# A hybrid decoder layer in f32: q as a ninth Strassen group, k and v with tokens on partitions

## The chip, the core and the metric

The kernel is one program on one core of one Trainium2 chip. A core has a matrix engine (PE, with PEld for its weight loads), a vector engine (DVE), a scalar engine (ACT), a general engine (POOL, which also issues DMAs in its own instruction stream) and a sync engine (SP, which only issues DMAs). The engines run their own instruction lists in order and wait for each other through semaphores. The metric is the device time of one execution in microseconds; lower is better.

## What is computed

The reference, cut to what matters (512 tokens, model width 2048, 16 query heads and 4 key heads of width 64, window 128):

```python
h = rms_norm(x, norm_gain)
z = h @ w_in                                   # columns: q k v g_attn c_b c_c c_h g_conv
q, k, v, g_attn, c_b, c_c, c_h, g_conv = jnp.split(z, SPLITS, axis=-1)
q = partial_rope(rms_norm(q, q_norm_gain), pos)     # per head; first 16 of 64 entries turn
k = partial_rope(rms_norm(k, k_norm_gain), pos)
y_attn = sliding_window_attention(q, k, v, sinks) * silu(g_attn)
y_conv = c_b * short_conv(c_c * c_h, conv_w) * silu(g_conv)
x = x + concatenate([y_attn, y_conv]) @ w_out
gate = sigmoid(rms_norm(x, ple_gate_norm_gain) @ w_ple_gate + b_ple_gate)
e = rms_norm(p @ w_ple_proj, ple_norm_gain)         # p: 512 x 256
out = x + gate * e
```

## The kernel before

**Three products for one.** Each f32 factor is split in a high part (a cast to fp32r on ACT) and a low part (the difference, on DVE). A product is three matmuls, high by high, high by low and low by high, 512 columns wide each. `wh` and `wl` are the parts of the weights, `hsh` and `hsl` those of h.

**Order.** Only PE's list is written out by hand throughout. In the first half of the program the other engines' lists are set by a scheduler (except for the first chunks); from the Strassen groups on all five lists stand in the order in which the code is written.

**First half.** (1) k and v: for each of 16 row blocks of x the block is scaled and split, and four tiles of k and v get three matmuls each, channels on partitions. (2) 16 tiles of 128 columns of w_in (`gemm_tile`, 48 matmuls each): eight of q, then eight of c_c and c_h. Between tiles lie, by a tick count (`at(when, fn)`, a tick is 6 matmuls), the attention of 16 pairs of key head and block, one `attention(j, n, when)` each, with `scores` at its tick, `turn` (transposes of the probabilities) 6 ticks later and `values` 9 ticks later. `q_tile` squares a tile of q, sums the squares per head by matmuls against `ind` (`half_sums`), turns them (`to_tokens`), and turns q by rope with four passes of DVE. (3) `e_block(n)`, the product of p and w_ple_proj, four times in the tiles of q. It needs the two tiles of p (`pt`), loaded through POOL's queue in `load_p` and split into `ptsh` and `ptsl`. (4) `h_forms` reads x again and makes, between the tiles, the sums of quarters of h that Strassen needs, and stores them in DRAM (`h_dram`).

**Second half.** Eight Strassen groups (`run_step`), 1024 columns of a product each: `g` 0 to 3 of w_in (the second halves of c_c and c_h; c_b and g_conv; g_attn), 4 and 5 of w_out, 6 and 7 of w_ple_gate. A group is 28 steps of 12 matmuls (7 products by 4 chunks) where the plain way takes 384. The weights of a step stand in the pools `wx`, `wy`, `ws`, are split two steps ahead (`prepare`), and their sums are made on DVE (`sums`) or by an accumulating DMA through POOL (`add_block`).

`rstd` makes 1 / sqrt on POOL, with an element-by-element power:

```python
nc.vector.tensor_scalar(ms, ms, 1.0 / n, EPS, op0=ALU.mult, op1=ALU.add)
nc.gpsimd.tensor_tensor(out, ms, e, op=ALU.pow)
```

Of the kernel before, what the change touches and what calls it, by code (L numbers as in the profile page):

```python
# [12 lines left out]
ALU = mybir.AluOpType  # L13

P = 128
# [12 lines left out]
NIN = 52  # L28
# [7 lines left out]
def hymba_layer(ctx: ExitStack, tc: tile.TileContext, io):  # L36
# [16 lines left out]
    ctx.enter_context(tc.manual_schedule(engines={mybir.EngineType.PE}))  # L53
# [5 lines left out]
    rowp = ctx.enter_context(tc.tile_pool(name="rowp", bufs=4, side="right", reuse_waits="tile"))  # L59
    ps_t = ctx.enter_context(tc.tile_pool(name="ps_t", bufs=2, space=PSUM))  # L60

    wide, early = ctx.enter_context(ExitStack()), ctx.enter_context(ExitStack())
    wsp = wide.enter_context(tc.tile_pool(name="wsp", bufs=4))
    wraw = wide.enter_context(tc.tile_pool(name="wraw", bufs=3))
    ps_g = wide.enter_context(tc.tile_pool(name="ps_g", bufs=2, space=PSUM, side="right"))
    big = early.enter_context(tc.tile_pool(name="big", bufs=31, side="right"))
    ps_s = early.enter_context(tc.tile_pool(name="ps_s", bufs=1, space=PSUM))
    ps_o = early.enter_context(tc.tile_pool(name="ps_o", bufs=1, space=PSUM))
    ps_m = early.enter_context(tc.tile_pool(name="ps_m", bufs=1, space=PSUM))
# [6 lines left out]

    E_AT = (2, 3, 4, 5)
    tiles = [TQ + i for i in range(8)]
    for i in range(4):
        tiles += [TCC + i, TCH + i]  # L80
    jobs = [io["w_kv"][i] for i in range(8)]
    for i, t in enumerate(tiles):
        jobs.append(io["w_in"][t, 0])
        if i in E_AT:
            jobs.append(io["w_ple_proj"][E_AT.index(i)])
        jobs.append(io["w_in"][t, 1])
    raws, splits = {}, {}
    RAW_AHEAD, SPLIT_AHEAD = 2, 3

    xt = []  # L90

    def load_x():
        xt.append(big.tile([P, T], F32, tag="big", name="x"))
        nc.sync.dma_start(xt[-1], io["x"][len(xt) - 1])

    def fetch(s):

        for j in range(min(s // 2 + RAW_AHEAD + 1, len(jobs))):
            if j not in raws:
                raws[j] = wraw.tile([P, 8, P], F32, name="raw")  # L100
                if j < 8:
                    for c in (slice(0, 4), slice(4, 8)):
                        nc.sync.dma_start(raws[j][:, c], jobs[j][:, c])
                        load_x()
                else:
                    nc.sync.dma_start(raws[j], jobs[j])

    def want(s, ahead):

        fetch(s)  # L110
        ahead = ahead if s > 5 else 0
        for j in range(min(s + ahead + 1, 2 * len(jobs))):
            if j not in splits:
                raw = raws[j // 2][:, (j % 2) * 4 : (j % 2) * 4 + 4]
                wh = wsp.tile([P, 4, P], F32R, name="wh")
                wl = wsp.tile([P, 4, P], F32R, name="wl")
                nc.scalar.copy(wh, raw)  # L117
                nc.vector.tensor_tensor(wl, raw, f32(wh), op=ALU.subtract)  # L118
                splits[j] = (wh, wl)
        return splits[s]  # L120

    tt, stt = nc.vector.tensor_tensor, nc.vector.scalar_tensor_tensor

    def split_tile(src, scale=None, name="s", pool=None):

        pool, tag = (big, "big") if pool is None else (pool, "h")
        h = pool.tile([P, T], F32R, tag=tag, name=name + "h")
        l = pool.tile([P, T], F32R, tag=tag, name=name + "l")
        if scale is None:
            nc.scalar.copy(h, src)  # L130
            nc.vector.tensor_tensor(l, src, f32(h), op=ALU.subtract)
        else:
            nc.scalar.activation(h, src, AF.Copy, scale=scale)
            nc.vector.scalar_tensor_tensor(l, src, scale, f32(h), op0=ALU.mult, op1=ALU.subtract)
        return h, l


    later = []
    clock = [0]

    def at(when, fn):
        later.append((when, len(later), fn))

    def tick():
        clock[0] += 1
        for item in sorted(x for x in later if x[0] <= clock[0]):
            later.remove(item)
            item[2]()

    def flush():  # L150
        while later:
            tick()

    def mm3(ps, wh, wl, ah, al, first, last):
        nc.tensor.matmul(ps, wh, ah, start=first, stop=False)  # L155
        nc.tensor.matmul(ps, wh, al, start=False, stop=False)  # L156
        nc.tensor.matmul(ps, wl, ah, start=False, stop=last)  # L157

    job = [0]

    def next_job(ahead=SPLIT_AHEAD):
        job[0] += 1
        return want(job[0] - 1, ahead)

    def gemm_tile(acts, mid=None):

        ps = ps_g.tile([P, T], F32, name="psg")
        for k in range(KT):
            if k == KT // 2 and mid:
                mid()  # L170
            if k % 4 == 0:
                wh, wl = next_job()
            ah, al = acts[k]
            mm3(ps, wh[:, k % 4, :], wl[:, k % 4, :], ah, al, k == 0, k == KT - 1)
            if k % 2:
                tick()
        return ps


    const.tile([P, 8], F32, name="pad")  # L180
    norm_g = const.tile([P, KT], F32, name="norm_gain")
    nc.scalar.dma_start(norm_g, io["norm_gain"])
    half_neg = const.tile([P, 32], F32, name="half_neg")
    nc.vector.memset(half_neg, -0.5)
    zeros = big.tile([P, P], F32, tag="big", name="zeros")
    nc.vector.memset(zeros, 0.0)
    nc.scalar.activation(half_neg[:, 31:], zeros[:, :1], AF.Copy, bias=-0.5)
    warm_ps = ps_o.tile([P, P], F32, name="pso")
    for _ in range(11):
        nc.tensor.matmul(warm_ps, zeros, zeros, start=True, stop=True)  # L190

    ind = const.tile([P, 2 * P], F32R, name="ind")
    for c in range(2):
        nc.vector.tensor_copy(ind[:, c * P : (c + 1) * P], zeros)
    ident = cload("ident", [P, P])
    gate_g = cload("ple_gate_norm_gain", [P, KT])
    qg, kg = cload("q_norm_gain", [P, 2]), cload("k_norm_gain", [P, 2])
    sink = cload("attn_sinks", [P, NH])
    convw = cload("conv_w", [P, 3, 8])
    nsink = const.tile([P, NH], F32, name="nsink")  # L200

    def half_sums(pm, hl, t, first, last):

        w = ind[:, P - 2 * t : 2 * P - 2 * t]
        nc.tensor.matmul(pm, w, hl[0], start=first, stop=False)
        nc.tensor.matmul(pm, w, hl[1], start=False, stop=last)

    def take_rows(pm, rows):
        sb = big.tile([rows, T], F32, tag="big", name="rowsum")
        nc.scalar.copy(sb, pm[:rows])  # L210
        return sb

    def to_tokens(sb):

        rows = sb.shape[0]
# [1201 lines left out]
```

## Time and profile before

| | |
|---|---|
| median of 3 runs | 937.83 us (936.92 to 941.45) |
| profiled execution | 936.5 us, its span 934.7 us |
| PE busy in the span | 922.9 us (99%) |
| DVE, ACT, POOL busy | 737.3, 533.5, 145.8 us |
| granted PE clock | 0.998 |
| moved by DMA | 188.22 MB |

The span runs from the first to the last instruction. "Busy" counts the time in which at least one instruction of an engine is under way, so that overlapping instructions count once. Matmuls overlap: one of 512 columns is under way for 390 ns, but the next starts long before it ends. A price per matmul is therefore read from the length of a run of them, not from the mean.

### The profile page before, as it was taken

The numbers are of one execution on the slowest core, as the hardware profiler recorded it, in microseconds if no ns is written. First come the engines' busy times: TensorE is split into PE (matmuls) and PEld (weight loads), VectorE is DVE, ScalarE is ACT, GpSimd is POOL, SyncE is SP. The second block draws the span as 40 slices with busy tenths as digits, with TensorE's granted clock in tenths as the row PEclk, the third lists the DMA queues.
The fourth block names the chain that finished last, engine by engine and source line by source line (L and its number), as shares of the span: only waits on it lengthen the run. The fifth ranks groups of instructions, "written<-read, shape, count | busy, mean of one in ns | idle before, by whom it ended". The sixth has DMA issues, their size and how long they took to land.

```text
span 934.7 us, 12298 instructions
## 1 busy us (share of the span) xinstructions
PE 922.9 (99%) x4264; PEld 765.9 (82%) x4264; DVE 737.3 (79%) x1115; ACT 533.5 (57%) x890; POOL 145.8 (16%) x190
## 2 busy tenths in 40 slices
PE   9999999999999899999999999999999999999997
PEld 8878888888888688888888888888888888888886
DVE  6776988888883877778667768989768696999778
ACT  7644856778883343445344446655657576565453
POOL 2002223154331000100100120011120112001100
PEclk9999999999999999999999999999999999999999
DMA  8524745556687677525924888795997996578747
GB/s 314 172 99 148 258 170 173 142 167 188 161 262 209 251 227 234 126 100 174 244 90 143 262 220 234 248 244 148 298 316 188 231 284 156 135 232 272 182 136 213
DMA packets 68590, 188.22 MB, mean 201 GB/s; under 512 B 8144, under 2 KB 14592, under 8 KB 68528
## 3 DMA queue, kind: packets, MB, share of 16 engines
q1 hardware_dynamic: 47312, 130.57, 40.6%
q0 software_dynamic: 21072, 56.86, 26.6%
q8 instruction: 33, 0.54, 0.2%
q14 instruction: 29, 0.24, 0.1%
q10 hardware_dynamic: 144, 0.01, 0.0%
HBM read 158.05 MB, written 29.36 MB: 200 GB/s over the span
## 4 chain that ended last, share of the span: by engine, by line
PE 96%; DVE 2%; issue 1%; ACT 0%; DVEq 0%
PE psp L853 60%; PE psg L155 6%; PE psg L156 6%; PE psg L157 6%; PE pst L853 3%; PE pss L276 2%; PE pst L276 2%; PE pst L919 2%; PE pst L484 1%; PE pss L564 1%; PE pst L564 1%; PE pss L451 1%; PE pss L452 1%; PE pso L499 1%; PE pso L498 1%
## 5 line engine op out<-in xcount | busy, mean ns | idle before, releaser
L853 PE MATMUL psp<-wh,form 128*128 128x512 f32 x1152 | 356.0, 390 | 0.0
L853 PEld LDWEIGHTS psp<-wh,form 128*128 128x128 f32 x1152 | 215.3, 188 | 44.1
L853 PE MATMUL psp<-wl,form 128*128 128x512 f32 x576 | 224.2, 389 | 0.0
L820 DVE TENSOR_TENSOR wl<-wy,wh 128x1024 fp32r<-128x1024 f32 x96 | 117.0, 1221 | 51.0 <-ACT wh L819 50.2
L819 ACT CAST wh<-wy 128x1024 fp32r<-128x1024 f32 x96 | 100.7, 1051 | 94.3 <-PE psp L853 69.3
L853 PEld LDWEIGHTS psp<-wl,form 128*128 128x128 f32 x576 | 108.1, 188 | 22.5
L820 DVE TENSOR_TENSOR wl<-wx,wh 128x1024 fp32r<-128x1024 f32 x64 | 78.1, 1222 | 40.8 <-ACT wh L819 40.6
L819 ACT CAST wh<-ws 128x1024 fp32r<-128x1024 f32 x64 | 67.5, 1054 | 71.6 <-PE psp L853 48.2
L819 ACT CAST wh<-wx 128x1024 fp32r<-128x1024 f32 x64 | 67.4, 1052 | 71.2 <-PE psp L853 58.5
L853 PE MATMUL psp<-wl,hsh 128*128 128x512 f32 x256 | 99.8, 390 | 3.4 <-DVE wl L820 3.4
L155 PE MATMUL psg<-hsh,wh 128*128 128x512 f32 x256 | 102.4, 400 | 0.0
L853 PE MATMUL psp<-wh,hsh 128*128 128x512 f32 x256 | 100.0, 391 | 0.0
L156 PE MATMUL psg<-hsl,wh 128*128 128x512 f32 x256 | 100.0, 391 | 0.0
L157 PE MATMUL psg<-hsh,wl 128*128 128x512 f32 x256 | 100.0, 390 | 0.0
L853 PE MATMUL psp<-wh,hsl 128*128 128x512 f32 x256 | 99.6, 389 | 0.0
L820 DVE TENSOR_TENSOR wl<-ws,wh 128x1024 fp32r<-128x1024 f32 x64 | 78.2, 1222 | 27.1 <-ACT wh L819 26.9
L805 DVE TENSOR_TENSOR wy<-wy,ws 128x1024 f32<-128x1024 f32 x64 | 77.9, 1218 | 0.0
L118 DVE TENSOR_TENSOR wl<-raw,wh 128x512 fp32r<-128x512 f32 x88 | 59.8, 685 | 17.7 <-PE pst L276 8.5
L117 ACT CAST wh<-raw 128x512 fp32r<-128x512 f32 x88 | 53.4, 614 | 30.2 <-PE psg L156 19.6
L853 PEld LDWEIGHTS psp<-wl,hsh 128*128 128x128 f32 x256 | 48.0, 188 | 13.8 <-DVE wl L820 3.8
L157 PEld LDWEIGHTS psg<-hsh,wl 128*128 128x128 f32 x256 | 48.1, 188 | 10.5
L853 PEld LDWEIGHTS psp<-wh,hsl 128*128 128x128 f32 x256 | 48.1, 188 | 9.9
(232 smaller groups left out, 1401.1 us busy)
## 6 DMA issues: line engine op xcount, KB each, us to landing
raw<-in_w_in SPq DMA_DIRECT2D x32, 512.0 KB, 3.7
ws<-in_w_mid SPq DMA_DIRECT2D x32, 512.0 KB, 4.3
wx<-in_w_mid SPq DMA_DIRECT2D x20, 512.0 KB, 4.2
h<-hf POOLq DMA_DIRECT2D x32, 256.0 KB, 4.6
wy<-in_w_mid SPq DMA_DIRECT2D x16, 512.0 KB, 7.4
wx<-in_w_out SPq DMA_DIRECT2D x16, 512.0 KB, 6.9
ws<-in_w_out SPq DMA_DIRECT2D x16, 512.0 KB, 5.5
ws<-in_w_ple_gate SPq DMA_DIRECT2D x16, 512.0 KB, 4.4
```

Source lines behind the costliest of these rows:

```text
L117: nc.scalar.copy(wh, raw)
L118: nc.vector.tensor_tensor(wl, raw, f32(wh), op=ALU.subtract)
L155: nc.tensor.matmul(ps, wh, ah, start=first, stop=False)
L156: nc.tensor.matmul(ps, wh, al, start=False, stop=False)
L157: nc.tensor.matmul(ps, wl, ah, start=False, stop=last)
L276: nc.tensor.matmul(kv_ps[t], w[:, t, :], a, start=k == 0 and i == 0, stop=k == KT - 1 and i == 2)
L564: nc.tensor.matmul(banks[t], a, w, start=k == 0 and i == 0, stop=k == 1 and i == 2)
L805: tt(y, y, got[g, "s1" if f == 6 else "s0", c], op=ALU.add)
L819: nc.scalar.copy(wh, src)
L820: tt(wl, src, f32(wh), op=ALU.subtract)
L853: nc.tensor.matmul(ps[t], a, w[:, i], start=start and first and i == 0 and n == 0, stop=last and i == 1 and n == 2, skip_group_check=not s ...
L919: nc.tensor.transpose(pt[:, b], quads[b // 2][:, b % 2, f * P : (f + 1) * P], ident)
```

## The change

The diff replaces the first half. What it does, part by part:

1. q is a ninth Strassen group (group 0 in the new count, the others move up by one). Its 28 steps stand between k and v and the tiles of c_c and c_h, and its result has tokens on partitions.
2. k and v are made with tokens on partitions (h as the stationary factor, 512 columns of weights moving), in eight chunks of two row blocks. Sums of squares per head are then sums along a row on DVE (`head_sums`), so `half_sums`, `to_tokens` and their `ind` go. Rope is made on POOL (`rope`, six instructions a time). k and q are turned by transposes afterwards (`make_k`, and `turn_q` in each unit of attention).
3. The forms of h are made during k and v from the x that is there (`form_sums`, `form5`, `form63`, and `form7` in group 0); x isn't read again for them. They feed group 0 and are stored in DRAM as before.
4. Attention doesn't scale the probabilities by 1 / sum; the reciprocals stay in `rs`, and the gate of the attention group is multiplied by them (`normalise`). Its `turn` stands 5 ticks and its `values` 7 ticks after `scores`, and the 16 units lie in 34 ticks of seven tiles (before: in some 60 of sixteen).
5. One set of pools for weights: the k and v weights stand in `ws`, x in `wy` and `quad`, the tiles of c_c and c_h in `wx`.
6. During k, v and group 0 all lists stand in written order; after group 0 the scheduler sets ACT, DVE, POOL and SP again, until the Strassen groups go on.

```diff
+    groups = [(io["w_mid"], n) for n in range(5)] + [(io["w_out"], n) for n in range(2)] + ...
+    T1_BY_DMA, T3_BY_DMA = (0, *range(2, NG - 1)), (4, 5, 6)
...
+    def rope(z, which, blocks):
+        nb, nh = z.shape[1], z.shape[2]
+        lo, hi = z[:, :, :, :half], z[:, :, :, half : ROT]
+        t = work_tile[0]("rope")[:, : 4 * nb * nh * half].rearrange("p (n b h d) -> p n b h d", n=4, b=nb, h=nh)
+        for n, src in enumerate((lo, hi, hi, lo)):
+            w = turns[which][:, n, blocks].unsqueeze(2).broadcast_to([P, nb, nh, half])
+            nc.gpsimd.tensor_tensor(t[:, n], src, w, op=ALU.mult)
+        nc.gpsimd.tensor_tensor(lo, t[:, 0], t[:, 1], op=ALU.subtract)
+        nc.gpsimd.tensor_tensor(hi, t[:, 2], t[:, 3], op=ALU.add)
...
+    def form_sums(j):
+        a11, a21, a12, a22 = (quarter_of(j, i, n) for n in range(2) for i in range(2))
...
+        tt(a22, a22, a21, op=ALU.subtract)
+        tt(g7[j // 2][:, j % 2 * 2 * P : (j % 2 + 1) * 2 * P], a11, a21, op=ALU.subtract)
+        stt(a11, a11, -1.0, a22, op0=ALU.mult, op1=ALU.subtract)
+        stt(a21, a12, -1.0, a11, op0=ALU.mult, op1=ALU.subtract)
...
+    for c in range(8):
+        if c > 1:
+            form63(c - 2) if c - 2 < 6 else None
+        if c < 7:
+            split_w(c + 1)
+            split_x(2 * c + 2)
+            split_x(2 * c + 3)
+        else:
+            prepare(1)
+        form_sums(c)
+        form5(c)
+        if c < 5:
+            load_kv()
+        elif c < 7:
+            load_more("xy")
+        for i in range(2):
+            k = 2 * c + i
+            for n, (a, w) in enumerate(((0, 0), (1, 0), (0, 1))):
+                for t in range(NB):
+                    nc.tensor.matmul(
+                        kv_ps[t // 2][:, t % 2], hs[k][a][:, t * P : (t + 1) * P], kv_split[c][w][:, i],
+                        start=k == 0 and n == 0, stop=k == KT - 1 and n == 2,
+                    )
...
+    def head_rstd(ms, r2):
+        tt(ms, ms, r2.unsqueeze(2).broadcast_to(ms.shape), op=ALU.mult)
+        rstd(ms, HD, ms)
...
+    def finish_q(t, n, junk):
...
+        def squares(b):
+            head_sums(z[:, b], ms[:, b], junk("sqq"))
+        def scale():
+            times_token(ms, tok["x"][:, blocks])
+            for b in range(2):
+                tt(z[:, b], z[:, b], ms[:, b].unsqueeze(2).broadcast_to([P, 8, HD]), op=ALU.mult)
+        return squares, lambda: head_rstd(ms, rx2_tok[:, blocks]), scale, lambda: rope(z, 0, blocks)
...
+    finish_early(0, 18, 18, 19, 22, 23)
+    finish_early(1, 22, 23, 24, 26, 27)
...
+    for s in range(PER):
+        run_step(s, hq)
+    qs[1, 0] = qtile("z")
+    take(qs[1, 0], 0, "a", 1.0)
...
+    for t in range(2):
+        squares, *then = finish_q(t, 0, mtile)
+        for b in range(2):
+            squares(b)
+        for fn in then:
+            fn()
...
+    at(2, rx2_rows)
+    at(4, lambda: make_k(1))
...
-                for r in range(4):
-                    if r < 2:
-                        nc.scalar.activation(t[:, r, lo:], t[:, r, lo:], AF.Copy, scale=sums[:, r : r + 1])
-                    else:
-                        nc.vector.tensor_scalar(t[:, r, lo:], t[:, r, lo:], sums[:, r : r + 1], None, op0=ALU.mult)
...
+        at(when - 3, turn_q)
+        at(when, scores)
+        at(when + 5, turn)
+        at(when + 7, values)
+        at(when + 11, lambda: cell["add"]())
...
+    load_p()
+    order = [(j, n) for j in (2, 3, 0, 1) for n in range(NB)]
+    for u, (j, n) in enumerate(order):
+        attention(j, n, 13 + 34 * u // 15)
+    mids = {0: {4: lambda: e_block(0), 8: lambda: e_block(1)}, 1: {0: lambda: e_block(2), 4: lambda: e_block(3)}}
...
+        def normalise(t, n):
+            for b in range(2):
+                z = q[t, n][:, b].rearrange("p (h d) -> p h d", d=HD)
+                tt(z, z, rs[:, 2 * t + b, 8 * n : 8 * n + 8].unsqueeze(2).broadcast_to([P, 8, HD]), op=ALU.mult)
```

The four parts of q after group 0 are `qs[t, n]`: 256 tokens by 512 columns. The last two, n = 0, are finished after the group's last step: `z_786` is t = 0 and `z_1379` is t = 1 in the lists below; `z_889` is the earlier part t = 1, n = 1. `msq` holds their sums of squares per head. The loads of p, `pt<-in_p`, stand here in POOL's list before the change, early in the program:

```order
L73 DMA conv_w_128<-in_conv_w 128x24
L311 DMA mask_621<-in_mask 128x256
L314 DMA cos_623<-in_cos 128x512
L315 DMA sin_624<-in_sin 128x512
L288 ISA
L288 TENSOR_SCALAR nsink_130<-attn_sinks_126 128x16
L676 MEMSET u_2354 128x2
L676 MEMSET u_2795 128x2
L537 DMA pt_697<-in_p 128x512
L537 DMA pt_703<-in_p 128x512
L229 TENSOR_TENSOR r_x_762<-ms_755,half_neg_98 128x4
L229 TENSOR_TENSOR msh_852<-msh_852,half_neg_98 128x16
```

And here in POOL's list after the change, where the program goes from group 0 to the tiles of c_c and c_h:

```order
L305 TENSOR_TENSOR msq_1419<-msq_1419,half_neg_172 128x16
L407 TENSOR_TENSOR rope_1432<-z_786,turn0_225 128x128 x4
L408 TENSOR_TENSOR z_786<-rope_1432 128x16x8
L409 TENSOR_TENSOR z_786<-rope_1432 128x16x8
L305 TENSOR_TENSOR msq_1439<-msq_1439,half_neg_172 128x16
L407 TENSOR_TENSOR rope_1452<-z_1379,turn0_225 128x128 x4
L834 DMA pt_1466<-in_p 128x512
L408 TENSOR_TENSOR z_1379<-rope_1452 128x16x8
L409 TENSOR_TENSOR z_1379<-rope_1452 128x16x8
L834 DMA pt_1472<-in_p 128x512
```

Ahead of the first row stands the rope of `z_889` (six instructions), the load of the mask and two memsets. The loads of p have moved behind these, two powers and most of two more ropes. DVE's list at the same place, before the change (the low parts of p, among the work on k and v):

```order
L118 TENSOR_TENSOR wl_723<-raw_576,wh_722 128x512
L343 TENSOR_TENSOR rot_647<-rot_647,shf_648 128x512
L118 TENSOR_TENSOR wl_746<-raw_576,wh_745 128x512
L131 TENSOR_TENSOR ptsl_700<-pt_697,ptsh_699 128x512
L131 TENSOR_TENSOR ptsl_706<-pt_703,ptsh_705 128x512
L243 TENSOR_REDUCE ms_755<-psm_756 128x4
```

And after it (`rb` feeds four transposes of PE, `vv` is v):

```order
L556 TENSOR_TENSOR msq_1419<-msq_1419,r_x_1082 128x16
L741 SCALAR_TENSOR_TENSOR vv_1461<-kv_714,r_x_1082,vv_1461 128x4x64
L579 TENSOR_TENSOR z_786<-z_786,msq_1419 128x512 x2
L548 TENSOR_REDUCE msq_1439<-sqq_1440 128x8
L548 TENSOR_REDUCE msq_1439<-sqq_1443 128x8
L552 TENSOR_TENSOR msq_1439<-msq_1439,rx2_tok_716 128x16
L300 TENSOR_SCALAR msq_1439<-msq_1439 128x16
L556 TENSOR_TENSOR msq_1439<-msq_1439,r_x_1082 128x16
L579 TENSOR_TENSOR z_1379<-z_1379,msq_1439 128x512 x2
L715 COPY rb_1497<-rx2_tok_716 128x512
L200 TENSOR_TENSOR ptsl_1469<-pt_1466,ptsh_1468 128x512
L200 TENSOR_TENSOR ptsl_1475<-pt_1472,ptsh_1474 128x512
```

The low parts of p, and ahead of them the rows for the transposes, now stand behind the finishing of the last two parts of q. PE's list at the first block of e, before (`psg` is a tile of q):

```order
L155 MATMUL psg_957<-hsh_351,wh_871 128x512
L156 MATMUL psg_957<-hsl_352,wh_871 128x512
L157 MATMUL psg_957<-hsh_351,wl_872 128x512
L564 MATMUL pss_996<-wh_892,ptsh_699 128x512
L564 MATMUL pss_996<-wh_892,ptsl_700 128x512
```

And after, 12 matmuls behind the end of group 0:

```order
L695 MATMUL psg_1478<-hsh_262,wh_1353 128x512
L695 MATMUL psg_1478<-hsl_263,wh_1353 128x512
L695 MATMUL psg_1478<-hsh_262,wl_1354 128x512
L718 MATMUL psm_1499<-ident_207,rb_1497 128x128 x4
L858 MATMUL pss_1513<-wh_1481,ptsh_1468 128x512
L858 MATMUL pss_1513<-wh_1481,ptsl_1469 128x512
```

The first block of e has moved from the third tile of q to the first third of the first tile after group 0.

1194 lines of the change are left out of this document (572 added, 622 removed).

## The prediction

> **What bounds the kernel now.** I read the page's busy times first, then PE's waits, then a table by stage, then the chain that ended last. Busy times of the span:
>
> ```profile
> PE 922.9 (99%) x4264; PEld 765.9 (82%) x4264; DVE 737.3 (79%) x1115; ACT 533.5 (57%) x890; POOL 145.8 (16%) x190
> ```
>
> PE is the bound, and only 11.8 us of the span are not its own. The waits of PE that have a named releaser, longest first:
>
> ```profile
> PE psp L853 <- DVE wl L820: 3.4, 1, 3.4
> PE pso L190 <- DVE zeros L186: 1.1, 1, 1.1
> PE pss L451 <- DVE negm L459: 0.7, 1, 0.7
> PE psm L219 <- ACT rowsum L210: 0.6, 1, 0.6
> ```
>
> The table by stage (k and v, the first tiles of q, attention's stretch, the entry to Strassen, the groups, the tail):
>
> ```profile
> core 0: us, PE busy (x) PEld busy (x) DVE busy (x) ACT busy (x) POOL busy (x), PEclk, DMA share, GB/s
> 5.90:49.50 43.60, 43.60 (x193) 36.12 (x192) 32.14 (x51) 28.86 (x51) 1.82 (x6) 1.00 0.70 245
> 49.50:150.00 100.50, 99.88 (x453) 81.19 (x452) 82.25 (x153) 58.49 (x118) 24.03 (x29) 1.00 0.51 172
> 150.00:299.20 149.20, 148.48 (x768) 124.49 (x767) 121.92 (x350) 111.36 (x302) 48.58 (x62) 1.00 0.62 180
> 299.20:312.00 12.80, 9.42 (x42) 7.49 (x41) 6.54 (x8) 3.14 (x3) 0.59 (x1) 1.00 1.05 374
> 312.00:910.00 598.00, 598.00 (x2713) 496.62 (x2712) 472.45 (x524) 319.89 (x401) 64.25 (x78) 1.00 0.71 205
> 910.00:934.70 24.70, 18.73 (x83) 15.19 (x81) 20.85 (x28) 8.70 (x11) 1.70 (x2) 0.93 0.67 202
> ```
>
> Everywhere PE is full: time saved must be PE's work, and any new wait of PE is time lost. The price of that work, from the chain (start, length, count):
>
> ```profile
> 311.59 76.05 PE psp L853 x334
> 387.64 0.87 PE pst L919 x8
> ```
>
> A matmul of 512 columns costs 76.05 / 334 = 0.228 us, a transpose 0.87 / 8 = 0.109.
>
> **What PE saves.** q costs 28 x 12 = 336 matmuls where eight tiles took 384: 48 fewer. The sums against `ind` go, 2 matmuls for each of 1 + 2 + 8 tiles: 22. Together 70 x 0.228 = 15.9 us. k, v, scores, values and the blocks of e keep their counts. Turning q and k takes 32 + 8 transposes more and 8 + 8 (of `rkb` and `vt`) go: +24, 2.6 us. The 16 small transposes of the row sums go:
>
> ```profile
> L219 PE MATMUL psm<-ident,rowsum 8*128 8x8 f32 (+2 forms) x16 | 1.6, 205 | 0.6 <-ACT rowsum L210 0.6
> ```
>
> They give 1.6. Net: -15.9 + 2.6 - 1.6 = -14.9 us on the bounding engine.
>
> **What PE waits for anew.** The first block of e stands 12 matmuls behind the end of group 0 (call it T), four transposes of `rb` before it. It needs both tiles of p. Before, these were loaded at 22 to 25 us (first row, of the tile) and used at 81 (second row, of the chain):
>
> ```profile
> L537 POOL DMA_DIRECT2D pt<-in_p x2: 544/576/607, 22.1 to 25.3; - x2
> ```
>
> ```profile
> 81.40 2.72 PE pss L564 x12
> ```
>
> Now their loads stand in POOL's list behind the finishing of q's last two parts, and `rb` and `ptsl` stand behind it on DVE. The prices, from the groups of instructions (count | busy us, mean ns of one | idle us before them and what ended it) and the DMA issues (KB, us to landing):
>
> ```profile
> L229 POOL TENSOR_TENSOR msh<-msh,half_neg 128x16 f32<-128x16 f32 x1 | 2.9, 2907 | 8.3 <-DVE msh L224 8.3
> L335 POOL TENSOR_TENSOR nscale<-msh,r_x 128x32 f32<-128x32 f32 x2 | 0.7, 369 | 0.1
> L288 POOL TENSOR_SCALAR nsink<-attn_sinks 128x16 f32<-128x16 f32 x1 | 0.3, 259 | 4.1 <-DMA attn_sinks<-in_attn_sinks 4.1
> L311 POOL DMA_DIRECT2D mask<-in_mask x1 | 0.5, 547 | 0.0
> pt<-in_p POOLq DMA_DIRECT2D x2, 256.0 KB, 6.0
> e<-e POOLq DMA_DIRECT2D x16, 256.0 KB, 3.8
> L820 DVE TENSOR_TENSOR wl<-wy,wh 128x1024 fp32r<-128x1024 f32 x96 | 117.0, 1221 | 51.0 <-ACT wh L819 50.2
> L819 ACT CAST wh<-wy 128x1024 fp32r<-128x1024 f32 x96 | 100.7, 1051 | 94.3 <-PE psp L853 69.3 <-DVE wy L801 6.2 <-PE pst L853 3.3
> L118 DVE TENSOR_TENSOR wl<-raw,wh 128x512 fp32r<-128x512 f32 x88 | 59.8, 685 | 17.7 <-PE pst L276 8.5 <-ACT wh L117 6.0 <-PE psm L254 1.7
> L117 ACT CAST wh<-raw 128x512 fp32r<-128x512 f32 x88 | 53.4, 614 | 30.2 <-PE psg L156 19.6 <-PE pst L276 9.4 <-DMA raw<-in_w_kv 1.1
> ```
>
> A power of 128x16 takes 2.9 on POOL. A step of rope on q (128 elements) has no row: no dearer than the 32 elements of L335 it costs 0.37, in proportion 1.48. From 16 elements (0.26) to 32 the price rises by 0.11, where proportion asks 0.26, so I take 0.6, and 3.6 for a rope of six. By the Trainium skill's "GPSIMD Engine Reference" (Performance versus the Vector engine) two-input arithmetic takes about 2.6 cycles of 1.2 GHz an element; 96 elements more than L335 then make an estimate of 0.58 a step; with it the sum below would be 0.3 lower.
>
> The chain: `wl_1510` stands ahead of the first power's input on DVE, and its buffer (one of three) is free only when PE ends the last step, T. Cast 1.05, difference 1.22, one small operation (0.2): T+2.5. POOL is meanwhile at the rope of `z_889` (scaled on DVE by about T-1), 3.6, and the mask's issue and two memsets, 0.75: free at T+3.4. Power: 6.3. DVE then has two small ones (0.6) and two scalings of 512 (1.4): 8.3. Rope of `z_786`: 11.9. The second power, whose input has long been ready: 14.8. DVE, small one and scalings: 16.4. Four steps of rope (2.4) and the first issue (0.6): 19.4; two more steps: 20.6; the second load lands 6.0 later, 26.6; cast and difference, 1.3: T+27.9. PE has 12 matmuls, four transposes and five products of the block to do by then, 4.3 us. So it stands 23.5 us. With the low prices throughout (0.37, landing 3.8) it is 17.5, in proportion 39; at 1.03 a step (the slope from 16 to 32 elements) 30.
>
> The stop also costs clock: the last row of the table, with 6 us idle, has 0.93 of full clock over 24.7 us, which is 1.7 us. I add 1.7 (0 to 3.4). The Trainium skill's "TensorE: Matmul & The Clock Gate" (Part 1) has a rule that speaks against any such stop: after an idle window of about 3.4 us the clock is halved until PE has been busy as long. By it the transposes of `rb` between two stops would take 0.4 us more as well, an estimate of 2.1 in place of 1.7, and the sum 0.4 higher.
>
> **The other parts.** Start: ACT casts both halves of the first weights before the first h, one cast more, 0.6 (0 to 1); I take 0.5. In k and v a chunk of 24 matmuls takes 5.5 us. ACT and DVE go in a ring there: ACT casts form 5 and forms 6 and 3, splits the weights, scales and casts two blocks; DVE takes the last difference and the first sum, which releases the next form 5.
>
> ```profile
> L585 ACT CAST form<-g 128x256 fp32r<-128x256 f32 x32 | 12.8, 404 | 4.8 <-DVE g L604 4.8
> L651 ACT ACTIVATE xg<-xg,norm_gain 128x512 f32<-128x512 f32 x16 | 11.4, 723 | 9.6 <-DMA xg<-in_x 9.5
> L604 DVE TENSOR_TENSOR g<-xg 128x256 f32<-128x256 f32 x8 | 3.4, 421 | 3.5 <-ACT xg L651 3.5
> ```
>
> 0.40 + 0.61 + 1.05 + 2 x (0.72 + 0.61) + 0.69 + 0.42 = 5.8, 0.3 over PE's, in six chunks: 2 us (0 to 6, since durations overlap a little, and waits between the engines add). DMA there: 8.4 MB of loads as before, 4 MB of forms stored and 4 MB of group 0's weights in some 45 us, 364 GB/s against 374 at most in the table; the weights come last, are due 11 us later, and I charge nothing (0 to 5).
>
> Attention now has 2.27 ticks a unit: PE 13.6 matmuls (3.1), scores (0.9 at half the price of 512 columns), 7 transposes, 3.5 value products, two transposes of q: 5.8 us. DVE's and ACT's parts:
>
> ```profile
> L459 DVE CUSTOM_DVE_ANT_0 prob<-pss,mask,nsink 128x256 f32<-128x256 f32 x48 | 23.7, 540 | 0.0
> L464 ACT ACTIVATE prob<-prob,negm 128x256 f32<-128x256 f32 x48 | 24.0, 500 | 10.6 <-DVE negm L459 10.6
> L464 ACT ACTIVATION_READ_ACCUMULATOR prob<-prob,negm 128x1 f32 x64 | 12.0, 187 | 0.0
> L501 ACT COPY up<-pso 128x512 f32<-128x512 f32 x16 | 9.1, 568 | 0.6 <-PE pso L499 0.6
> L459 DVE DVE_READ_ACCUMULATOR2_ANT negm<- 128x1 f32 x64 | 5.3, 83 | 0.0
> L471 DVE RECIPROCAL sums<-sums 128x4 f32<-128x4 f32 x16 | 2.8, 176 | 0.4
> ```
>
> DVE: 4 x 0.62 (with 0.08 of reading) + 1.75 x 0.69 (low parts of the probabilities) + two differences of q 0.84 + three small ones 0.5 + weights 0.57 x 1.22 + conv, four passes of 0.69 in seven units, 0.4 = 6.1. ACT: 4 x 0.69 + 1.75 x 0.61 + 0.57 + two casts of q 0.8 + a small one 0.2 + weights 0.6 = 6.0. Added up as durations both are over PE's 5.8, by 0.3 x 16 = 5 us; overlapped as now they are under. I take 2 (0 to 8). Attention's own scalings, 32 on ACT and 32 on DVE, were in no wait of PE; leaving them out, and the eight multiplications of `normalise` in a group where DVE has 20% to spare, count nothing. The h forms were beside full PE too: nothing. The 3.4 us at the entry to Strassen came from DVE waiting for attention's last stores; these end two ticks earlier now, but the `wy` loads wait for them: -1.7 (-3.4 to +3).
>
> **Sum.** 936.5 (the profiled execution; the median is 1.3 above it) - 14.9 + 23.5 + 1.7 + 0.5 + 2 + 2 - 1.7 = 949.6.
>
> **Rivals.** First, the other side: POOL's loads go out past its arithmetic. For it speaks only that a load needs nothing of the powers; against it, that POOL's issues stand in the trace as instructions of its own, 0.55 us each. Then only `rb` holds PE. It is done at T+16.8, a stop of 14, with 940 us; if the first part's power is also done before T, rb comes at T+8, a stop of 5, and 931. Faster begins at a stop of about 7. Second: the stop is there, and attention or k and v become bound by DVE and ACT besides (their tops, +6 and +4): 960. For it speak 6.1 and 6.0 against 5.8; against it 82% and 75% in the same stretch now. That Strassen saves less than counted I don't weigh: the 48 matmuls are in the list.
>
> **Chances.** Forecast 0.65 (0.56 slower, 0.09 with the low prices within 0.5%), first rival 0.22 (0.12 faster, 0.10 the same), second 0.13. Slower by over 0.5% 0.69, within 0.5% 0.19, faster 0.12; 0.5%, 4.7 us, is about what this kernel's measurement can tell. Range 932 to 968: below it the first rival's faster end, above it 1.03 a step together with the other tops. The forecast's own range is 939 to 963.
>
> **What would show it.** Right: one wait of PE of some 20 us at the first block of e, released by the low part of p (DVE), after one at the transposes of `rb`; the loads of p issued after T+15; group 0 at 76 to 78 us; PE busy about 908. Wrong: the loads of p before T, waits spread through attention, or steps of rope far from 0.6.

## The result

The changed kernel takes 964.7 us (963.4 to 965.9), the kernel before beside it 937.5: a ratio of 1.028, 95% interval 1.025 to 1.031. The forecast was 950, so the direction came out, and the size at less than half: +12 against +27. One execution of one of the experiments (the kernel with part (1, 1) of q late) took 3131 us and is left out of its median. The profiled execution took 965.9 us, its span 964.0. First the busy times:

```profile
PE 919.2 (95%) x4202; PEld 757.5 (79%) x4202; DVE 731.8 (76%) x1039; ACT 532.8 (55%) x856; POOL 180.2 (19%) x250
```

PE issued 62 instructions fewer (4264 to 4202), which is the -70 + 24 - 16 of the count in the forecast. The matmuls saved are there; 95% where there were 99% says that waits took more than they gave. These are the waits of PE in the changed kernel that are 2 us or more in sum (us in total, times, longest):

```profile
PE psm L718 <- issue: 18.3, 1, 18.3
PE pss L858 <- ACT ptsh L199: 4.1, 1, 4.1
PE pss L773 <- DVE negm L779: 3.7, 3, 2.5
PE psp L241 <- DVE wl L200: 3.6, 5, 1.9
PE psp L241 <- ACT wh L199: 2.6, 2, 2.0
PE pst L977 <- DVE z L1065: 2.4, 2, 2.1
```

L718 is the transposes of `rb`, L858 the first block of e, L773 the scores, L241 a Strassen step, L977 the transposes of the gate. "issue" beside 18.3 us means that the profile found no releaser; the rows below show that it is the copy of `rb` on DVE. The table by stage (k and v; group 0; the first tile with the first blocks of e; two parts of attention's stretch) says where they lie:

```profile
core 0: us, PE busy (x) PEld busy (x) DVE busy (x) ACT busy (x) POOL busy (x), PEclk, DMA share, GB/s
6.99:51.63 44.64, 44.01 (x192) 36.04 (x193) 36.54 (x67) 34.14 (x53) 13.83 (x27) 1.00 0.98 350
51.63:138.51 86.88, 80.50 (x338) 63.27 (x336) 65.49 (x86) 52.92 (x92) 37.37 (x53) 0.98 0.59 194
138.51:170.00 31.49, 9.10 (x30) 6.29 (x29) 12.88 (x24) 5.44 (x8) 18.48 (x26) 0.62 0.27 87
170.00:230.00 60.00, 57.49 (x276) 47.25 (x275) 43.69 (x96) 40.30 (x103) 12.14 (x21) 0.97 0.48 165
230.00:327.12 97.12, 95.40 (x520) 79.85 (x519) 65.93 (x199) 63.88 (x182) 27.68 (x33) 1.00 0.54 118
```

The third stretch holds the stop that was forecast: 9.1 us of PE's work in 31.5. The second holds what was not: group 0 takes 86.9 us where 336 matmuls at 0.228 are 76.5. DMA is at 0.98 all through k and v.

**The stop.** POOL's list behind the end of group 0 (T = 138.5):

```profile
136.55 2.91 POOL L305 TENSOR_TENSOR msq<-msq,half_neg 128x16 f32<-128x16 f32 x1
141.55 3.85 POOL L407 TENSOR_TENSOR rope<-z,turn 128x128 f32<-128x128 f32 x4 [2.09 <-DVE z L579]
147.42 2.94 POOL L305 TENSOR_TENSOR msq<-msq,half_neg 128x16 f32<-128x16 f32 x1
152.25 1.69 POOL L407 TENSOR_TENSOR rope<-z,turn 128x128 f32<-128x128 f32 x4 [1.89 <-DVE z L579]
154.84 2.91 POOL L305 TENSOR_TENSOR msq<-msq,half_neg 128x16 f32<-128x16 f32 x1
159.43 1.73 POOL L407 TENSOR_TENSOR rope<-z,turn 128x128 f32<-128x128 f32 x4 [1.68 <-DVE z L579]
161.11 0.61 POOL L834 DMA_DIRECT2D pt<-in_p x1
```

and DVE's, with two of its waits for powers and the copy that PE waits for:

```profile
150.39 0.18 DVE L556 TENSOR_TENSOR msq<-msq,r_x 128x16 f32<-128x16 f32 x1 [4.71 <-POOL msq L305]
...
157.78 0.18 DVE L556 TENSOR_TENSOR msq<-msq,r_x 128x16 f32<-128x16 f32 x1 [3.82 <-POOL msq L305]
157.99 1.29 DVE L579 TENSOR_TENSOR z<-z,msq 128x512 f32<-128x512 f32 x2
159.20 0.42 DVE L715 COPY rb<-rx_tok 128x512 f32<-128x512 f32 x1
```

Powers of 2.9 us, each with DVE waiting for it (1.4 us for the first, 4.7 and 3.8 in the rows), and each followed by a rope; the first load of p goes out at 161.1, T + 22.6. `rb` is done at 159.6, T + 21.1 (forecast T + 16.8), PE goes on 0.1 us later, and stops again until the first high part of p lets it go on at T + 26.4 (forecast, for the last low part, T + 27.9).

**Group 0.** ACT ahead of the longest wait there, and PE's first matmuls behind it:

```profile
84.12 0.63 ACT L534 ACTIVATE xp<-xp 128x512 f32<-128x512 f32 x1 [2.69 <-DMA xp<-in_x_tok]
...
85.36 1.03 ACT L199 CAST wh<-wy 128x1024 fp32r<-128x1024 f32 x1
```

```profile
86.44 0.73 PE L241 MATMUL psp<-wh,form 128*128 128x512 f32 x2 [2.00 <-ACT wh L199]
```

`xp` is x by tokens, 4 MB read a second time in group 0 for the sums of squares of a token. ACT squares it, and the cast of the next weights stands behind these squares in ACT's list. The load comes late (the DMA engines are busy at 1.00 from 74 to 85 us), the squares wait, the cast waits, PE waits. The trace alone does not say whether the load, ACT's work or the weights' own loads are the cause; the experiments do.

### The profile page after: what moved, and what is told of

The parts are those of the page before. It is cut to its first block, busy times and chain, and to the rows that moved or that the text cites. A ratio compares the mean times of both kernels' runs of the same rounds, so it can differ in the third digit from the quotient of the medians.

```text
span 964.0 us, 12104 instructions
## 1 busy us (share of the span) xinstructions
PE 919.2 (95%) x4202; PEld 757.5 (79%) x4202; DVE 731.8 (76%) x1039; ACT 532.8 (55%) x856; POOL 180.2 (19%) x250
## 4 chain that ended last, share of the span: by engine, by line
PE 64%; DVE 2%; DMA 1%; ACT 0%; issue 0%; SPq 0%; DVEq 0%
PE psp L241 57%; PE pst L241 3%; PE pst L977 2%; DMA e<-e 1%; PE pst L1330 1%; PE psg L695 1%; DVE wl L200 0%; DVE wy L189 0%; DVE z L1065 0%; DVE form L200 0%; DVE z L1230 0%; ACT z L983 0%; DVE z L323 0%; ACT wh L199 0%; PE pso L810 0%
## 5 line engine op out<-in xcount | busy, mean ns | idle before, releaser
L241 PE MATMUL psp<-wh,form 128*128 128x512 f32 x1280 | 396.4, 391 | 2.0 <-ACT wh L199 2.0
L241 PEld LDWEIGHTS psp<-wh,form 128*128 128x128 f32 x1280 | 239.9, 188 | 51.6 <-ACT wh L199 2.4
L241 PE MATMUL psp<-wl,form 128*128 128x512 f32 x640 | 250.4, 391 | 0.8 <-DVE wl L200 0.7
L241 PEld LDWEIGHTS psp<-wl,form 128*128 128x128 f32 x640 | 120.5, 188 | 27.8 <-DVE wl L200 2.4
L241 PE MATMUL psp<-wl,hsh 128*128 128x512 f32 x304 | 119.3, 393 | 2.9 <-DVE wl L200 2.9
L241 PE MATMUL psp<-wh,hsh 128*128 128x512 f32 x304 | 119.7, 394 | 0.7 <-ACT wh L199 0.6
L241 PE MATMUL psp<-wh,hsl 128*128 128x512 f32 x304 | 119.0, 392 | 0.0
L241 PEld LDWEIGHTS psp<-wl,hsh 128*128 128x128 f32 x304 | 57.5, 189 | 16.5 <-DVE wl L200 4.4
L241 PEld LDWEIGHTS psp<-wh,hsh 128*128 128x128 f32 x304 | 57.4, 189 | 13.1 <-ACT wh L199 1.5
L241 PEld LDWEIGHTS psp<-wh,hsl 128*128 128x128 f32 x304 | 57.5, 189 | 11.8
L200 DVE TENSOR_TENSOR wl<-raw,wh 128x1024 fp32r<-128x1024 f32 (+1 forms) x29 | 34.5, 1188 | 16.5 <-ACT wh L199 16.4
L695 PE MATMUL psg<-hsh,wh 128*128 128x512 f32 x112 | 46.7, 417 | 0.0
L695 PE MATMUL psg<-hsh,wl 128*128 128x512 f32 x112 | 44.2, 395 | 0.0
L695 PE MATMUL psg<-hsl,wh 128*128 128x512 f32 x112 | 44.1, 393 | 0.0
```

The costliest lines, as they stand in the source:

```text
L200: tt(l, src, f32(h), op=ALU.subtract)
L241: nc.tensor.matmul(ps[t], a, w[:, i], start=start and first and i == 0 and n == 0, stop=last and i == 1 and n == 2, skip_group_check=not s ...
L695: nc.tensor.matmul(ps, w[:, k % 8], a, start=k == 0 and n == 0, stop=k == KT - 1 and n == 2)
```

## The experiments

**Two causes in one stop.** Theory A: `rb` behind the powers on DVE, and p behind powers and ropes on POOL, are two holds in a row. Two kernels take away one each:

```diff
# e1_p_first: load_p() ahead of finish_q of the last two parts, and
-            nc.gpsimd.dma_start(pt, io["p"][k])
+            nc.sync.dma_start(pt, io["p"][k])
# e2_rb_first: the copy rb ahead of finish_q of the last two parts, p as it was
+    rb = mtile("rb").rearrange("p (b t) -> p b t", t=P)
+    nc.vector.tensor_copy(rb, rx2_tok.unsqueeze(2).broadcast_to([P, NB, P]))
     for t in range(2):
         squares, *then = finish_q(t, 0, mtile)
```

> Edit: the two tiles of p are loaded through SP's queue, and the code of their loads and splits stands ahead of the finishing of q's last two parts; rb stays where it is. Theory A (the stop at the first block of e has two causes in a row, each by an engine's list in order: rb behind two waits for powers on DVE, and p's loads behind powers and ropes on POOL): the first wait of PE (transposes of rb, 18.3 us) stays within 1.5 us, the second (4.1 us, low part of p) goes; 964.7 - 4.1 - 0.5 of clock = 960, 958 to 962. Rival B (p's loads alone hold PE, rb's place on DVE is a by-product): both waits go, 22 us less, 942. Rival C (the loads wait for memory that group 0's weight buffers still hold, so the queue doesn't matter): 963 to 966, loads of p still issued after 150 us.

> Edit: the copy rb, which the transposes on PE read, stands in the code ahead of the finishing of q's last two parts; p is loaded as in the changed kernel. Theory A: PE passes the transposes of rb without a wait (or under 1 us) and stops at the block of e until the low part of p is there, at about 26 us behind the end of group 0 as now; one wait of some 21 to 22 us in place of 18.3 + 4.1, time the same within 2 us, 963 to 966. Rival B' (rb alone holds PE and p's loads only look late): 964.7 - 18 to 22 = 943 to 947.

Measured: 960.2 us and 964.8. PE's longest wait with p early, and with `rb` early:

```profile
PE psm L733 <- issue: 18.6, 1, 18.6
```

```profile
PE pss L858 <- ACT ptsh L199: 22.6, 1, 22.6
```

With p early the wait for `rb` stays and the second goes; with `rb` early the wait for p grows to 22.6 and nothing is won. Both holds are shown, and each covers the other, so that mending one shows 4.5 us or nothing. Rivals B, B' and C are out.

**The common cause moved away.** The finishing of q's last two parts goes to ticks 6 to 17 of the second stage, once with p where it was, once with p early as well:

```diff
-    for t in range(2):
-        squares, *then = finish_q(t, 0, mtile)
-        ...
...
+    finish_late(0, 6, 8, 10, 11)
+    finish_late(1, 12, 14, 16, 17)
```

> Edit: the finishing of q's last two parts (squares, two powers, scalings, rope) stands at ticks 6 to 17 of the second stage (a tick is 6 matmuls) instead of ahead of it; loads of p stay on POOL's queue. Theory A: nothing waits for a power ahead of rb, which is there at about 2 us behind the end of group 0; p's loads stand behind only the rope of the part before (ends 8 us behind the end of group 0), land 3 us later, and are split by 13 us behind it; PE has 4.3 us of work: a stop of 8 to 9 in place of 22.4, and some 1 us less of clock: 964.7 - 14 - 1 = 950, 946 to 953. Rival D (the late rope of q is then late for the eighth unit of attention, and the stop comes back there): above 955, with a wait of PE at the transposes of q.

> Edit: both, the finishing of q's last two parts at ticks 6 to 17 and the loads of p through SP's queue ahead of them. Theory A: the whole stop of 22.4 us and the 2.4 us of half clock behind it go: 964.7 - 24.8 = 940, 938 to 943, and what is left over the time before is group 0's loss of 10 us, attention's 4 and normalise's 2.4. Rival D as above: a new wait at the transposes of q in attention, above 945. Rival E (DVE and ACT, now without the pause, are the bound of the first tiles): waits of 5 us or more at the blocks of e, 945 to 950.

Measured: 950.9 and 946.9. The first has the time expected, but by another route; POOL's issue of p, and PE's longest waits in it:

```profile
140.39 1.26 POOL L842 DMA_DIRECT2D pt<-in_p  x2
```

```profile
PE pss L866 <- ACT z L320: 4.4, 1, 4.4
PE psm L769 <- DVE st L774: 3.8, 2, 2.4
```

The stop at the block of e is 4.4 us and not 8 to 9, since the loads of p went out ahead of the early part's rope, which still waited for its scaling; what PE waits for there is the last eviction of group 0, which stands in ACT's list behind the casts of p. Another 3.8 us came up further on, at the transposes of q. The second missed 940 by 7 us. Three of its waits of PE, and DVE's for powers in the same stretch:

```profile
PE psm L783 <- DVE st L788: 3.3, 2, 2.0
PE pss L866 <- DVE ptsl L200: 2.5, 2, 1.3
...
PE pss L866 <- DVE e L859: 1.8, 1, 1.8
```

```profile
DVE msq L556 <- POOL msq L305: 6.6, 3, 3.1
```

The 22.4 us are gone, but 7.6 come back: DVE still stands behind each power that POOL makes, now in the middle of the blocks of e and of attention. That is half rival D (the transposes of q) and half rival E.

**Group 0, one suspect at a time**, on top of that kernel (946.9). For these the lengths in the traces decide, since they were timed on another occasion than the base, and the two differ by as much as some of the effects (the kernel before took 939.2 us beside the base and 936.8 beside these). In the six traces whose group 0 has the same code (the changed kernel, the first four experiments and the last of these) it takes 86.4 to 87.6 us; that is the scatter to set the lengths against.

```diff
# e6_small_xp: of x by tokens 64 of 512 columns, read seven times by ACT; it leaves out seven eighths of the sum of squares
-            nc.sync.dma_start(xpart[t, n], tokens[:, 2 * t : 2 * t + 2, n * T : (n + 1) * T])
+            nc.sync.dma_start(xpart[t, n][:, :, :64], tokens[:, 2 * t : 2 * t + 2, n * T : n * T + 64])
...
# e7_form7_stores_late: form 7's stores
-        nc.gpsimd.dma_start(h_dram[j][i], f32(flat(s)))
+            soon(after, 16 + j // 2, nc.sync.dma_start, h_dram[j][i], f32(flat(s)))
# e8_q11_late: squares of part (1, 1) behind group 0, the rest at ticks 1 and 4
-    finish_early(1, 22, 23, 24, 26, 27)
+    squares, *then = finish_q(1, 1, mtile)
# e9_normalise_earlier
-        soon(after, s0 + 22, lambda: normalise(1, 1))
+        soon(after, s0 + 21, lambda: normalise(1, 1))
```

> Base: the kernel with the finishing late and p first (946.9 us). Edit: of x by tokens only 64 of 512 columns are loaded in group 0 (0.5 MB instead of 4 MB), and ACT's squares read these 64 seven times, 448 elements each, so that ACT's work is nearly the same; it leaves out seven eighths of the sum of squares, and what follows has other values but the same instructions. Theory F (ACT's casts of weights stand in its list behind squares that wait for late loads of x by tokens): the waits of PE for wh at 84 and 99 us behind the start (2.0 and 0.6), those for wl that follow at once (0.5 and 0.5) and the half clock behind the first go: group 0 some 6 us shorter, 941, 939 to 943. Rival G (ACT has too much work there, whatever the loads do): waits stay, 945 to 947. Rival H (the weights' own loads are late because of the accumulating loads and the stores of the forms): waits stay and move to ws or wy, 945 to 947.

> Base: the kernel with the finishing late and p first (946.9 us). Edit: the eight stores of form 7 (2 MB) go out through SP's queue at steps 16 to 19 of group 0 instead of POOL's at steps 6 to 10, where the loads of x by tokens run. Theory F with DMA full as the reason that the loads are late: the load that took 9 us lands in 6 to 7, the wait of PE for wh at 84 us shrinks from 2.0 to under 1 or goes: 3 to 5 us less, 942 to 944. Rival I (the loads are late because SP's list issues them late, behind tiles that come free late, whatever else is in flight): 946 to 948.

> Base: the kernel with the finishing late and p first (946.9 us). Edit: the third part of q (tokens 256 to 511, heads 8 to 15) is squared, scaled and turned in the second stage (ticks 0 to 4) instead of at steps 22 to 27 of group 0. Theory J (DVE is overfull in the last eight steps: two sums, two scalings of 0.6 to 0.7 us, small ones of 0.2 to 0.4, and it shares time with POOL's ropes): the waits of PE for wl at 127 and 133 us (1.9 and 0.5, 2.5 to 3 us with the slower start behind them) go, and the second stage pays at most 1 us of it back: 944 to 945.5. Rival K (the work only moves, and is in the way of the blocks of e): 946 to 949, waits of PE at the blocks of e above 4 us.

> Base: the kernel with the finishing late and p first (946.9 us). Edit: in the group of g_attn the scaling of the part (1, 1) by the reciprocals stands one step earlier on DVE, behind its silu at once instead of behind the next step's weights. Theory L (the wait of 2.4 us of PE at the transposes of the gate is this scaling, queued behind a sum and a difference of weights): the wait goes, 944.5, 943.5 to 945.5. Rival M (DVE is full there, and PE then waits for the weights instead): 946 to 947.5.

| kernel | us | group 0, us (from its first matmul to the first of the next tile) |
|---|---|---|
| changed kernel | 964.7 | 86.9 |
| base (finishing late, p first) | 946.9 | 86.4 |
| small loads of x by tokens | 941.9 | 80.9 |
| stores of form 7 late | 943.9 | 83.4 |
| part (1, 1) of q late | 945.6 | 84.9 |
| scaling one step earlier | 945.7 | 87.6 |

What ACT's squares waited for the loads (us, times), and the loads' time to landing; in the base, with form 7's stores late, and with the small loads:

```profile
  DMA xp<-in_x_tok: 6.3, 3
...
DMA to landing us min/median/max: 3.8/6.2/9.2
```

```profile
  DMA xp<-in_x_tok: 3.4, 5
...
DMA to landing us min/median/max: 4.3/5.2/6.2
```

```profile
  DMA xp<-in_x_tok: 2.0, 4
...
DMA to landing us min/median/max: 1.8/3.0/6.3
```

With the small loads no wait of PE for `wh` is left. So the chain is shown from both ends: with an eighth of the bytes group 0 is 5.5 us shorter at nearly the same work of ACT, and with 2 MB of other traffic moved out of the way the longest landing falls from 9.2 to 6.2 us and 3 of the 5.5 us come. Rival G is out, since ACT has nearly the same work, and rival I, since moving the stores alone shortens group 0. Rival H, late loads of the weights themselves, is out as well: ACT's casts of weights wait 2.7 us for their own loads in the changed kernel and 3.5 with the small loads of x, and there PE waits for no cast.

Part (1, 1) of q taken out of group 0 shortens it by 1.5 us, and the tiles of c_c and c_h behind it take 1.8 us longer (171.6 against 169.8). PE's wait for the scaling of e grows there from 1.8 us to 4.3, with matmuls at half rate behind it, while the 2.5 for `ptsl` go:

```profile
PE pss L873 <- DVE e L866: 4.3, 1, 4.3
```

```profile
143.63 0.17 DVE L556 TENSOR_TENSOR msq<-msq,r_x 128x16 f32<-128x16 f32 x1 [3.95 <-POOL msq L305]
...
164.71 0.18 DVE L556 TENSOR_TENSOR msq<-msq,r_x 128x16 f32<-128x16 f32 x1 [3.05 <-POOL msq L305]
```

PE's wait ends at 172.3 us. DVE stands 4 us behind the power of that part (second row), has little idle time after it, and stands 3 us behind the next part's power (third row, as in the base) shortly before e's scaling. How much of the 4.3 us each power causes, no run separates. Theory J is right in part: of the two waits for `wl` that were to go, the one of 0.5 us went, and the other is 1.3 us where the base has 1.4. Rival K has the wait right (above 4 us), and the time, 945.6, lies between the two. The earlier scaling does away with its wait of 2.4 us, and leaves 1.0 for weights in its place; from the first matmul of group 1 to the end the trace is 1.7 us shorter (308.6 to 945.4, 636.9, against 310.1 to 945.3, 635.2). In the total (945.7 against 946.9) that can't be told, so theory L rests on one trace, and rival M holds for the 1.0.

**All together.** The first adds the mends, with each load of x by tokens three steps ahead of its squares instead of two, and the steps that need their sums one step later. The second besides keeps DVE out of every power's way: what follows a power stays on POOL.

```diff
# v1_fixes, besides the edits above
-        soon(after, 7 + i // 2 * 2, load_xpart, *divmod(i, 4))
-        soon(after, 9 + i // 2 * 2, square_xpart, *divmod(i, 4))
+        soon(after, 7 + i // 2 * 3, load_xpart, *divmod(i, 4))
+        soon(after, 10 + i // 2 * 3, square_xpart, *divmod(i, 4))
...
# v2_q_on_pool, besides: part (1, 1) of q behind group 0, rb ahead of p's loads; for the three later parts of q, eng is POOL
-    def finish_q(t, n, junk):
+    def finish_q(t, n, junk, eng=None):
+        mul = (eng or nc.vector).tensor_tensor
...
-            times_token(ms, tok["x"][:, blocks])
+            mul(ms, ms, tok["x"][:, blocks].unsqueeze(2).broadcast_to(ms.shape), op=ALU.mult)
             for b in range(2):
-                tt(z[:, b], z[:, b], ms[:, b].unsqueeze(2).broadcast_to([P, 8, HD]), op=ALU.mult)
+                mul(z[:, b], z[:, b], ms[:, b].unsqueeze(2).broadcast_to([P, 8, HD]), op=ALU.mult)
...
-            nc.gpsimd.dma_start(e_dram[t // 2][n][:, t % 2], e)
+            nc.sync.dma_start(e_dram[t // 2][n][:, t % 2], e)
```

> All mends so far in one: the kernel with the finishing late and p first, form 7's stores late, the scaling of part (1, 1) a step earlier, and besides each load of x by tokens stands three steps ahead of its squares on ACT instead of two. If the causes add: 946.9 - 3 (stores of form 7) - 2.4 (scaling) - 2.4 (the rest of what the small loads of x gave) = 939, 937 to 941, as fast as before. If the later squares only push the powers and ropes of k and q behind the end of group 0 (rival): 941 to 944, with waits of PE at the transposes of k or q.

> As the one before, and besides: the three later parts of q are finished in the second stage, with their token product and scalings on POOL instead of DVE, rb ahead of p's loads in the code, and the stores of e through SP. Theory: DVE never waits for a power, so that the waits at the blocks of e (ptsl 2.5, e 1.8), at the transposes of q (3.3) and the late weights at the end of group 0 (some 2.5) go: 939 - 7 to 9 = 930 to 932, faster than before by 0.6 to 0.8%. Rival (POOL's chain of some 9.5 us a part, three parts, ends too late for the third and the ninth unit of attention): a wait of PE at the transposes of q of 5 us or more, 937 to 942.

Measured: 940.3 us, ratio 1.0016 (0.9993 to 1.0038), the same as before; and 932.9 us, ratio 0.9937 (0.9916 to 0.9957), 0.6% faster than before and 1 us above the 930 to 932 expected. The longest wait of the first, 3.4 us, is again at the transposes of `rb`, which stands behind a power on DVE there (DVE waits 4.2 us for it). Group 0 takes 79.6 us in the one and 76.6 in the other, the 76.5 of the count. The busy times and longest waits of the second:

```profile
PE 912.7 (98%) x4202; PEld 754.3 (81%) x4202; DVE 727.3 (78%) x1030; ACT 531.9 (57%) x856; POOL 175.1 (19%) x233
```

```profile
PE pss L806 <- DVE negm L812: 4.5, 3, 3.3
PE pss L877 <- DVE ptsl L200: 1.4, 1, 1.4
```

DVE has no wait for a power left in group 0 and the tiles behind it. Of the 7.6 us at the transposes of q and the blocks of e 3.1 are left (0.6 + 1.4 + 1.1), while the waits for `negm` rise from 2.7 us in the first to 4.5. What is left to win first is the longest of these (3.3 us), at the scores.

## Why the prediction was half right

The sum of the forecast against the trace, both for the profiled executions (936.5 to 965.9, spans 934.7 to 964.0: +29.3 where +13.1 was forecast):

| term | forecast | measured |
|---|---|---|
| PE's work | -14.9 | -62 instructions, as counted (-14.9 at the same prices) |
| start | +0.5 | +1.1 (first matmul at 6.99, before 5.91) |
| k and v | +2 | +1.0 (192 matmuls 44.6, before 43.6) |
| waits in group 0, with slow matmuls behind them | 0 | +10.4 (6.2 of waits) |
| stop at the first block of e | +23.5 | +22.4 |
| clock behind it | +1.7 | +3.1 |
| attention | +2 | +2.9 of waits (4.2, before 1.3), some 1.5 of slow restart |
| entry to Strassen | -1.7 | -3.4 (the wait is gone) |
| scaling by the reciprocals | 0 | +2.4, some 1.7 of slow restart |

(The clock behind the stop: from T to 169.25 PE did 12 matmuls, four transposes and nine matmuls, 5.2 us of work at full rate, in 30.7 us, with 22.4 us of waits.) Added up that is +28.2; some 1 us of the 29.3 has no place. PE's busy time fell to 919.2 us and not to the 908 that the forecast gave as a sign of being right: a matmul at half rate is under way for 0.63 us instead of 0.39. In group 0 PE is busy for 80.5 us where the count gives 76.5, and in the stretch of the stop for 9.1 where it gives some 6.

- **Right: the stop.** Its place, its two waits, their order and the sum of the two (23.5 against 22.4) came out, and by the mechanism named. How it divides was off: the sign asked for some 20 us at the first block of e, though the forecast's own chain, with `rb` at T + 16.8, leaves PE some 14 there and 9 at the block of e; the runs have 18.3 and 4.1, and the second ends with the high part of p, not the low one. That the sum is so near is in part luck, since two errors cancel. The early part's power ended at T + 1 and not ahead of T (first row of POOL's list), so that POOL was free at T + 9 instead of T + 3.4, and all behind it was 4 to 5.5 us later; in return the first load of p was there 3.1 us after its issue (161.1, ACT's cast at 164.2), where 6.0 was taken, with the DMA engines busy at 0.27 in that stretch. Steps of rope took 0.66 (first four), 0.71 and 0.46 us in the mean of all ropes of q, where 0.6 was chosen: 3.8 a rope against 3.6. The three behind T took 4.9, 2.6 and 2.7 us, the first beside a busy DVE.
- **The step that failed** is "DMA there ... the weights come last, are due 11 us later, and I charge nothing (0 to 5)", and with it "group 0 at 76 to 78 us". The weights' own loads cost PE nothing that the runs show. The loads that came late were those of x by tokens, which the prediction did not list: 4 MB on DMA engines that were full, and on ACT the squares that wait for them with the casts of weights behind. It cost some 5.5 of the 10.4 us (what the small loads gave). Of the rest, DVE late with `wl`, 1.5 us went when one early part of q left group 0, and 3.0 when it did so with the loads mended (79.6 to 76.6); the prediction had looked at this work only behind T. The reasoning that gave the stop, an engine's list in order with all that stands behind a wait, was not applied to ACT in group 0.
- **Also undersized**: "the eight multiplications of normalise ... count nothing". DVE did have 20% to spare, but the scaling stood behind a sum and a difference of weights and one step ahead of its reader. Spare time in the mean does not help an instruction with a deadline.
- **Rivals.** The first (loads go past POOL's arithmetic) is refuted: the issue at 161.1 stands in POOL's list above, in the middle of the last rope. The second (attention bound besides) holds in part, 4.2 us of waits, one of them 2.5 us long, at 220 us, where DVE's list had passes of conv and a difference of weights ahead of the maxima.
- The range (to 968) holds the time for another reason than the one its top was made for: dear ropes and tops of attention and k, v, where it was group 0.

## What to carry to other kernels

When work moves to an engine that is off the critical path, write out what its list and the lists that wait for it look like at the place where PE is next due: a value that a slow engine makes (a power, 2.9 us) also stops every later instruction of the engine that takes it, so keep the steps that follow on the slow engine itself or place them where their taker has nothing due behind them. List every transfer of a stretch, also those that feed no matmul: one late load in front of the casts of weights on an engine holds up the weights too. And two holds in a row hide each other: mending one shows next to nothing until both are gone.

## What the runs showed of the hardware

**A pause of 2 us can be enough for half the clock, and isn't always.** Transposes of the gate in the changed kernel, the wait of 2.1 us, and the matmuls behind it:

```profile
628.78 0.30 PE L977 MATMUL pst<-ident,z 128*128 128x128 f32 x1 [2.11 <-DVE z L1065]
...
630.34 0.63 PE L241 MATMUL psp<-wh,hsl 128*128 128x512 f32 x1
630.77 0.63 PE L241 MATMUL psp<-wl,hsh 128*128 128x512 f32 x1
...
633.61 0.39 PE L241 MATMUL psp<-wh,hsh 128*128 128x512 f32 x1
633.83 0.39 PE L241 MATMUL psp<-wh,hsl 128*128 128x512 f32 x1
```

To 633.3 they start 0.43 us apart, behind that 0.22 to 0.23. The same shows behind the pauses of 2.0 + 0.5 us at 84 us and of 2.5 at 220, and not behind the one of 1.85 at 127. Where it shows, such a pause costs some 1.5 to 2 us more, and the stop of 22.4 us cost no more than 3.1. But the length alone doesn't decide. The same wait of 2.1 us at the gate has matmuls 0.23 us apart right behind it in two of the experiments (p early; part (1, 1) late), a pause of 1.85 us at 128 us in the kernel with only the finishing late has eight at half rate, and the longest wait of the kernel before has next to nothing behind it:

```profile
311.59 0.50 PE L853 MATMUL psp<-wl,hsh 128*128 128x512 f32 x1 [3.38 <-DVE wl L820]
311.94 0.40 PE L853 MATMUL psp<-wh,hsh 128*128 128x512 f32 x1
```

These start 0.35 us apart, and the next ones 0.22 to 0.24. The Trainium skill's "TensorE: Matmul & The Clock Gate" (Part 1) gives the idle window as about 3.4 us and advises against pauses above that; here shorter ones were enough in some traces, and one of 3.4 us was not in another. That the same pause costs clock in one trace and none in the next would fit its account of a window that runs free of the kernel; no run here shows the window itself.

**Small steps of POOL waited out DVE's two-input instructions.** Two steps of rope on POOL, 32 elements each, beside two differences and sums of weights on DVE; behind them the same step beside a row sum on DVE:

```profile
122.07 1.28 DVE L189 TENSOR_TENSOR wy<-wy,ws 128x1024 f32<-128x1024 f32 x1
123.27 1.27 DVE L200 TENSOR_TENSOR wl<-wy,wh 128x1024 fp32r<-128x1024 f32 x1
```

```profile
122.34 1.12 POOL L408 TENSOR_TENSOR kv<-rope 128x32 f32<-128x32 f32 x1
123.42 1.23 POOL L409 TENSOR_TENSOR kv<-rope 128x32 f32<-128x32 f32 x1
...
126.66 0.25 POOL L408 TENSOR_TENSOR kv<-rope 128x32 f32<-128x32 f32 x1
```

The slow steps end 0.1 us behind the end of DVE's instruction (123.46 against 123.35, 124.65 against 124.54), and the step is 0.25 us beside the one-input sum. The Trainium skill's "GPSIMD Engine Reference" (Key points) says that POOL shares its SBUF interfaces with DVE and contends with instructions of two SBUF inputs; the rows agree, and add the price: such a small step cost nearly the whole of DVE's instruction, 1.1 to 1.2 us for 0.25. It isn't so for every instruction of POOL: the power at 136.55 took its 2.91 us though a two-input difference of DVE ran for 1.2 us of it, while two others, beside more of DVE's, took 3.8.
